# GEGLU MLP, first pass: weight quads from the third on by casting DMA, and half of w_down kept on chip until the down phase

## The chip, the cores and the metric

The kernel runs on one core of a Trainium2 chip. The metric is the device time of one launch in microseconds. A profile is one execution of its own, and its span is about 2 us shorter than the time reported for the same run.

## The reference

Eight batches of 1024 rows (8192 rows in all) of width 1024 go through a gated MLP with an intermediate width of 4096:

```python
gate = x @ w_gate                       # (8192, 1024) @ (1024, 4096)
up = x @ w_up
gate = 0.5 * gate * (1 + np.tanh(np.sqrt(2 / np.pi) * (gate + 0.044715 * gate ** 3)))
h = gate * up
return (h @ w_down).astype(np.float32)  # (8192, 4096) @ (4096, 1024)
```

## The kernel before

The kernel takes the rows in eight passes of 1024. Each pass has a gate/up phase and a down phase. Both multiply block matrices with seven products instead of eight, so sums of weight blocks are operands too, and VectorE makes them. In the first three passes the gate/up phase runs over 16 *pairs* of 14 products; one product is four matmuls of 128x128 by 128x512. A *quad* is the 512 columns of both weights that serve two pairs. Later passes use operands that passes two and three have stored.

The first pass has two extra duties. It has to bring the weights in as fp16 while there is no spare memory, and it has to make the 14 chunks of w_down operands (seven blocks in two halves) that every down phase loads.

Weights, first pass: ScalarE loads eighths of a quad in fp32 and casts them. The casting load of the next two passes is shown with it.

```python
def load_stage(u):                                  # issued on ScalarE
    q, w, k = eighth(u)
    if q < NQ:
        nc.scalar.dma_start(out=staging(u), in_=w_v[w][:, k, q * 512 : (q + 1) * 512])

def cast_stage(u):
    q, w, k = eighth(u)
    if q < NQ:
        nc.scalar.copy(raw(0, q)[:, w, k], staging(u))

def load_raw(p, q):                                 # passes 1 and 2: fp32 to fp16 in the DMA
    if q < NQ:
        for w in range(2):
            nc.gpsimd.dma_start(out=raw(p, q)[:, w], in_=w_v[w][:, :, q * 512 : (q + 1) * 512])
```

w_down, first pass: eight groups, each of four casting loads from GpSimd's queue into one staging tile (`h_s`), four sums on VectorE and seven stores from SyncE's queue.

```python
def wd_load(q, t):
    nc.gpsimd.dma_start(out=hf["s3"][:, t * 1024 : (t + 1) * 1024], in_=wd_v[:, 4 * q + t, :])
# ... wd_sums(k): four sums of 128x1024 on VectorE
def wd_store(q):
    # ...
    for v, src in ((0, b11), (1, b21), (5, b22), (2, tt[:, 0]), (3, tt[:, 1]), (4, tt[:, 2]), (6, tt[:, 3])):
        nc.sync.dma_start(out=dst(v), in_=src)
```

Where they stand, counted in products from the start of the pass (14 to a pair):

```python
for u in range(8):                                   # every quad
    s = (3, 6, 9, 12, 14, 16, 18, 20)[u] + (2 if q == 0 else 0)
    # ... cast eighth 8*(q+1)+u, then load the eighth four further on
for n in range(8):
    s0 = 24 * n + 6
    for ds, f, a in (
        (0, wd_load, (n, 0)), (2, wd_load, (n, 1)), (4, wd_load, (n, 2)), (6, wd_load, (n, 3)),
        (14, wd_sums, (0,)), (15, wd_sums, (1,)), (16, wd_sums, (2,)), (17, wd_sums, (3,)),
        (19, wd_store, (n,)),
    ):
        # ...
```

## Time and profile before

| what | us |
|---|---|
| median of all runs up to the prediction's result (4) | 2335.75 |
| profiled span | 2331.6 |
| TensorE idle in the span | 48 |
| first gate/up pass, pairs 2 to 15 | 194.4 |
| the same 784 matmuls at the second pass's rate | 169.3 |

How to read the profile lines: PE is TensorE, DVE VectorE, ACT ScalarE, POOL GpSimd and SP SyncE; a q behind the name is the engine's sequencer, which among other things issues DMAs. L462 is line 462 of the kernel (the changed kernel has other numbers). `ps` is PSUM, the memory that TensorE writes its products to, used here as eight banks; `tmp` are the temporaries that ScalarE copies them to; `h_s` is the staging tile of w_down and `wd_ops` its operands in device memory. "PE ps L462 <- ACT tmp L473: 11.3, 10, 4.8" says that TensorE waited 11.3 us in all for ScalarE's copy, in 10 waits, the longest 4.8 us.

### The profile page before, as it was taken

To read this page: it belongs to the slowest core of one execution; us is meant where nothing else is said; L and a number is where in the kernel's file an instruction comes from. 1 tells how busy PE (TensorE), PEld (TensorE's weight loads), DVE (VectorE), ACT (ScalarE), POOL (GpSimd) and SP (SyncE) were. 2 spreads that over 40 slices of the span, in tenths; PEclk is the share of its full clock that TensorE was granted. 3 is DMA by queue.
4 is the path that set the end of the run, shared out by engine and by line. 5 is a ranking of instruction groups with operands and counts; after the bars stand their busy time and mean duration, and the time that the engine had idled before them with its cause. 6 is when DMAs were issued, how large, how long until landed. Compare 5 with 4: busy or idle time off the path is not lost.

```text
span 2331.6 us, 38269 instructions
## 1 busy us (share of the span) xinstructions
PE 2283.6 (98%) x14668; PEld 1434.6 (62%) x14668; DVE 1348.8 (58%) x1959; ACT 1015.2 (44%) x1922; POOL 668.6 (29%) x813
## 2 busy tenths in 40 slices
PE   6899999999999999999999999999999999999999
PEld 2334444444444444888558884688747886488854
DVE  4556536775377772576627674466734667356650
ACT  5666215553155530555215551255413654055530
POOL 1222102331033310444205450145402543034520
PEclk9999999999999999999999999999999999999999
DMA  8899778989799885897768876798857988588852
GB/s 268 244 272 275 224 184 206 224 215 296 183 212 257 204 292 200 279 317 271 236 223 289 305 278 207 254 306 288 275 195 260 319 275 265 198 275 276 268 215 108
DMA packets 259942, 579.22 MB, mean 248 GB/s; under 512 B 76016, under 2 KB 119024, under 8 KB 244976
## 3 DMA queue, kind: packets, MB, share of 16 engines
q1 hardware_dynamic: 206080, 490.80, 61.8%
q0 software_dynamic: 38448, 56.63, 14.5%
q10 hardware_dynamic: 15232, 29.36, 3.8%
q8 instruction: 114, 1.87, 0.3%
q14 instruction: 68, 0.56, 0.1%
HBM read 520.09 MB, written 113.25 MB: 272 GB/s over the span
## 4 chain that ended last, share of the span: by engine, by line
PE 90%; DMA 4%; ACT 2%; DVE 1%; issue 1%; ACTq 0%; POOL 0%; SPq 0%; DVEq 0%; POOLq 0%
PE ps L671 39%; PE ps L766 33%; PE ps L462 18%; DMA ring<-in_w_up_dram 1%; ACT ring L260 1%; DMA h_s<-in_w_down_dram 1%; DMA wd_ops<-h_s 1%; ACT tmp L473 1%; DMA h_a<-in_w_gate_dram 1%; DMA h_a<-in_w_up_dram 0%; DVE ring L295 0%; ACTq L253 0%; DMA w_ops<-x_sums 0%; DVE tmp L481 0%; DVE h_a L499 0%
## 5 line engine op out<-in xcount | busy, mean ns | idle before, releaser
L671 PEld LDWEIGHTS <-ring 128*128 128x128 f16 x8320 | 814.1, 98 | 95.2
L648 POOL TENSOR_TENSOR h_a<-tmp 128x256 f16<-128x256 f32 x640 | 465.1, 747 | 927.7 <-ACT tmp L636 893.4
L766 PE MATMUL ps<-ring,h_a 128*128 128x512 f16 x3072 | 665.6, 379 | 0.0
L671 PE MATMUL ps<-x_sums,ring 128*128 128x256 f16 x5760 | 655.8, 273 | 0.0
L633 DVE TENSOR_TENSOR tmp<-tmp,ps 128x512 f32<-128x512 f32 x640 | 413.8, 683 | 219.5 <-PE ps L671 167.9
L766 PEld LDWEIGHTS <-h_a 128*128 128x128 f16 x3072 | 300.6, 98 | 361.4
L462 PEld LDWEIGHTS <-ring 128*128 128x128 f16 x2688 | 263.5, 98 | 354.5 <-issue 42.0
L618 ACT COPY tmp<-ps 128x512 f32<-128x512 f32 x520 | 304.8, 586 | 203.1 <-PE ps L671 130.2
L462 PE MATMUL ps<-x_sums,ring 128*128 128x512 f16 x1536 | 355.4, 381 | 24.9 <-ACT tmp L473 14.4
L636 ACT ACTIVATE tmp<-tmp 128x256 f32<-128x256 f32 x640 | 264.1, 418 | 172.8 <-DVE tmp L631 80.3
L722 ACT ACTIVATE tmp<-ps 128x512 f32<-128x512 f32 x128 | 76.4, 597 | 587.2 <-PE ps L766 587.2
L671 PE MATMUL ps<-x_b,ring 128*128 128x256 f16 x2560 | 305.6, 273 | 0.0
L488 POOL TENSOR_TENSOR h_a<-tmp 128x512 f16<-128x512 f32 x96 | 153.0, 1593 | 435.8 <-ACT tmp L486 332.8
L462 PE MATMUL ps<-x_b,ring 128*128 128x512 f16 x1152 | 265.9, 380 | 2.4 <-ACT ps L478 2.0
L631 DVE TENSOR_TENSOR tmp<-ps,tmp 128x512 f32<-128x512 f32 x240 | 165.4, 689 | 152.2 <-ACT tmp L618 104.8
L726 DVE SCALAR_TENSOR_TENSOR tmp<-ps,tmp 128x512 f32<-128x512 f32 x64 | 44.2, 690 | 305.7 <-ACT tmp L722 262.6
L481 DVE TENSOR_TENSOR tmp<-ps,tmp 128x512 f32<-128x512 f32 x192 | 129.4, 683 | 155.0 <-ACT tmp L473 153.3
L730 DVE TENSOR_TENSOR h_a<-h_a,h_a 128x2048 f16<-128x2048 f16 x96 | 111.1, 1216 | 64.6 <-PE ps L766 64.6
L473 ACT COPY tmp<-ps 128x512 f32<-128x512 f32 x192 | 111.7, 586 | 84.4 <-PE ps L462 71.3
L295 DVE TENSOR_TENSOR ring<-ring 128x1024 f16<-128x1024 f16 x192 | 137.4, 729 | 8.9 <-DMA ring<-in_w_up_dram 8.6
L486 ACT ACTIVATE tmp<-tmp 128x512 f32<-128x512 f32 x96 | 60.3, 628 | 137.5 <-DVE tmp L481 135.6
L766 PE MATMUL ps<-ring,h_s 128*128 128x512 f16 x512 | 111.8, 379 | 0.0
(57 smaller groups left out, 790.3 us busy)
## 6 DMA issues: line engine op xcount, KB each, us to landing
ring<-w_ops SPq DMA_DIRECT2D x480, 512.0 KB, 4.5
ring<-wd_ops SPq DMA_DIRECT2D x112, 1024.0 KB, 5.1
out_dram<-tmp SPq DMA_DIRECT2D x128, 256.0 KB, 2.8
w_ops<-x_sums SPq DMA_DIRECT2D x110, 256.0 KB, 6.3
w_ops<-h_s SPq DMA_DIRECT2D x82, 256.0 KB, 5.7
ring<-in_w_gate_dram POOLq DMA_DIRECT2D x16, 1024.0 KB, 9.8
ring<-in_w_up_dram POOLq DMA_DIRECT2D x16, 1024.0 KB, 18.1
wd_ops<-h_s SPq DMA_DIRECT2D x56, 256.0 KB, 5.8
```

The source lines that it names most:

```text
L295: nc.vector.tensor_tensor(o, a, b, op)
L462: nc.tensor.matmul(ps(b, w), lhs[:, k], rhs[:, k, :], start=(first and k == 0), stop=(k == KH - 1), skip_group_check=True,)
L473: nc.scalar.copy(tl((n, w)), ps("a", w))
L481: nc.vector.tensor_tensor(o, ps("b", w), o, ADD)
L488: nc.gpsimd.tensor_tensor(hq[TO[n]][:, i, :], tmp[:, t[n, 1]], tmp[:, t[n, 0]], MUL)
L618: nc.scalar.copy(tmp[:, t[o[1]]], ps_all[:, bank[o[2]]])
L631: nc.vector.tensor_tensor(d, b, a, SUB)
L633: nc.vector.tensor_tensor(d, a, b, ADD if o[4] == "add" else SUB)
L636: nc.scalar.activation(d, d, GELU, scale=GSC)
L648: nc.gpsimd.tensor_tensor(h, tmp[:, t[o[1]], MQ : 2 * MQ], g, MUL)
L671: nc.tensor.matmul(ps_all[:, bank[c], w * MQ : (w + 1) * MQ], lhs[:, w, k], rhs[:, k], start=(first and w == 0 and k == 0), stop=(k == KH ...
L766: nc.tensor.matmul(ps_all[:, bank[b, g]], lhs[:, j, g * P : (g + 1) * P], dc[:, n, :], start=(first and j == 0), stop=(j == NP - 1), skip_ ...
```

## The change

Its intent is to free ScalarE in the first pass, and to halve the work of making the w_down operands there. The weights from the third quad on come by the casting DMA that the later passes use. Of w_down, only half is staged in the gate/up phase (four groups instead of eight); the other half is loaded at the end of the phase into memory that has become free, and its sums and stores are made during the first down phase.

```diff
     def load_stage(u):
         q, w, k = eighth(u)
-        if q < NQ:
+        if q == 1:
@@ gate_up_one, first pass
-                for u in range(8):
-                    s = (3, 6, 9, 12, 14, 16, 18, 20)[u] + (2 if q == 0 else 0)
+                for u in range(8 if q == 0 else 0):
+                    s = (5, 8, 11, 14, 16, 18, 20, 22)[u]
@@
-                for n in range(8):
-                    s0 = 24 * n + 6
+                if e == 1:
+                    at(13, load_raw, p, q + 2)
+                if 11 <= i < 15:
+                    at(7, half_load, 0, 2 * (i - 11))
+                if i >= 14:
+                    at(4, half_load, 1, 4 * (i - 14))
+                    at(6, half_load, 1, 4 * (i - 14) + 2)
+                for n in range(4):
+                    s0 = 36 * n + 34
@@ down, first pass (cut: half_sum, half_store, half_block and their places)
+        half_work = {
+            (0, 1): [lambda: half_sum(1, 0)],
+            (0, 3): [lambda: half_sum(1, 1)],
+            ...
+            (2, 0): [lambda: half_store(0), lambda: half_store(1)],
+            ...
+        }
@@
+                if p == 0:
+                    if kc == 0:
+                        for k in (2, 4, 6):
+                            load_d(p, k)
+                    load_d(p, {0: 8, 6: 10, 8: 12}.get(kc, 14))
```

More of the change, by code (lines that the diff above doesn't have):

```diff
@@ L131 @@
     wd_v = w_down.rearrange("(nc n) h -> n nc h", n=P)
+    wd_eo = w_down.rearrange("(j e n) h -> e n j h", e=2, n=P)
     xh = nc.dram_tensor("x_half", (M, K), FP16, kind="Internal").ap()
@@ L258, in cast_stage @@
         q, w, k = eighth(u)
-        if q < NQ:
-            nc.scalar.copy(raw(0, q)[:, w, k], staging(u))
+        nc.scalar.copy(raw(0, q)[:, w, k], staging(u))
     def staging0(w, kh):
@@ L373, in wd_store, with half_load, half_block, half_sum @@
             nc.sync.dma_start(out=dst(v), in_=src)
-    order = [[]]
-    def d_chunk(k):
-        o = 4096 * order[0][k % 6]
+    wd_half = [
+        t.rearrange("p (j h) -> p j h", j=8) for t in (xc[:, 8192:16384], rg[:, 0:8192])
+    ]
+    wd_t = [xc[:, j * 4096 : (j + 1) * 4096].rearrange("p (j h) -> p j h", j=8) for j in range(2)]
+    def half_load(e, j):
+        nc.gpsimd.dma_start(out=wd_half[e][:, j : j + 2], in_=wd_eo[e][:, 8 + j : 10 + j, :])
+    def half_block(v):
+        lo, hi = slice(0, HH), slice(HH, 2 * HH)
+        return (
+            wd_half[0][:, :, lo], wd_half[1][:, :, lo], wd_t[1], wd_t[0],
+            wd_half[0][:, :, hi], wd_half[1][:, :, hi], wd_half[0][:, :, lo],
+        )[v]
+    def half_sum(n, r):
+        b11, b21, t2, t1, b12, b22, _ = [half_block(v)[:, 4 * r : 4 * r + 4] for v in range(7)]
+        o, a, b = ((t1, b12, b11), (t2, b22, t1), (b12, b22, b12), (b11, b21, t2))[n - 1]
+        nc.vector.tensor_tensor(o, a, b, SUB)
+    def half_store(v):
+        nc.sync.dma_start(out=wdop[2 * v + 1], in_=half_block(v))
+    order = [[]]
+    def d_place(p, k):
+        if p == 0:
+            return (4, 2, 3, 5, 4, 5, 4)[k // 2]
+        return order[0][k % 6]
+    def d_chunk(p, k):
+        if p == 0 and k % 2:
+            return half_block(k // 2)
+        o = 4096 * d_place(p, k)
         return rg[:, o : o + 4096].rearrange("p (n h) -> p n h", n=8)
-    def load_d(k):
-        if k < 14:
-            nc.sync.dma_start(out=d_chunk(k), in_=wdop[k])
+    def load_d(p, k):
+        if k < 14 and (p or k % 2 == 0):
+            nc.sync.dma_start(out=d_chunk(p, k), in_=wdop[k])
     SEQ = [
@@ L524, in gate_up_one @@
             if p == 0:
-                for u in range(8):
-                    s = (3, 6, 9, 12, 14, 16, 18, 20)[u] + (2 if q == 0 else 0)
+                for u in range(8 if q == 0 else 0):
+                    s = (5, 8, 11, 14, 16, 18, 20, 22)[u]
                     if s // 14 == e:
                         k = s % 14 + 1
-                        at(k, cast_stage, 8 * (q + 1) + u)
-                        at(k, load_stage, 8 * (q + 1) + u + 4)
+                        at(k, cast_stage, 8 + u)
+                        at(k, load_stage, 8 + u + 4)
                 if first:
@@ L565, in gate_up_one @@
                 order[0] = [0, 1, 4, 2, 3, 5] if p % 2 == 0 else [2, 3, 4, 0, 1, 5]
-                at(2, load_d, 0)
-                at(3, load_d, 1)
+                if p:
+                    at(2, load_d, p, 0)
+                    at(3, load_d, p, 1)
             if i == NP - 1:
-                at(1, load_d, 2)
+                at(1, load_d, p, 2 if p else 0)
             pair(p, i, extra, SEQ0 if first else SEQ, AFTER0 if first else AFTER1)
@@ L683, in quad @@
                 if q == NQ - 1 and j % 2 == 1:
-                    load_d(j // 2)
+                    load_d(p, j // 2)
             for f in extra.get(n, ()):
@@ L738, in down @@
             sums["P6", 0, r] = [("a12", "a12", "a11", SUB, r)]
+        half_work = {
+            (0, 1): [lambda: half_sum(1, 0)],
+            (0, 3): [lambda: half_sum(1, 1)],
+            (1, 1): [lambda: half_sum(2, 0)],
+            (1, 3): [lambda: half_sum(2, 1)],
+            (2, 0): [lambda: half_store(0), lambda: half_store(1)],
+            (3, 0): [lambda: half_store(2)],
+            (3, 1): [lambda: half_sum(3, 0)],
+            (3, 3): [lambda: half_sum(3, 1)],
+            (4, 0): [lambda: half_store(3)],
+            (5, 0): [lambda: half_store(5)],
+            (5, 1): [lambda: half_sum(4, 0)],
+            (5, 3): [lambda: half_sum(4, 1)],
+            (6, 0): [lambda: half_store(4)],
+            (7, 0): [lambda: half_store(6)],
+        }
         work = deque()
@@ L759, in down @@
                 kc = 2 * v + nb
-                dc = d_chunk(kc)
+                dc = d_chunk(p, kc)
                 for g in range(G):
@@ L802, in down @@
                         hsum(*s)
+                    if p == 0:
+                        for f in half_work.get((kc, g), ()):
+                            f()
                     if nb == 0 and g == 0 and p + 1 < NPASS:
@@ L810, in down @@
                         work.popleft()()
-                if kc == 0:
-                    for k in range(3, 6):
-                        if p < FAST:
-                            load_d(k)
-                load_d(kc + 6)
+                if p == 0:
+                    if kc == 0:
+                        for k in (2, 4, 6):
+                            load_d(p, k)
+                    load_d(p, {0: 8, 6: 10, 8: 12}.get(kc, 14))
+                else:
+                    if kc == 0 and p < FAST:
+                        for k in range(3, 6):
+                            load_d(p, k)
+                    load_d(p, kc + 6)
                 if p + 1 < FAST:
```

## The prediction

> **What bounds the kernel now.** I read the summary page first. It says that TensorE is the bound nearly everywhere:
>
> ```profile
> PE 2283.6 (98%) x14668; PEld 1434.6 (62%) x14668; DVE 1348.8 (58%) x1959; ACT 1015.2 (44%) x1922; POOL 668.6 (29%) x813
> ```
>
> PE is busy for 2283.6 of 2331.6 us. All that any change to waits can win is the other 48 us, plus stretches at a low clock. The next view is the table by stretches. I chose the boundaries from the matmuls' timeline: the first two pairs of the first gate/up pass, its other fourteen pairs, and the whole gate/up of the second pass.
>
> ```profile
> 34.30:62.60 28.30, 24.38 (x106) 10.27 (x105) 16.61 (x25) 18.26 (x26) 4.74 (x4) 0.96 0.77 247
> 62.60:255.40 192.80, 174.38 (x778) 76.44 (x777) 117.08 (x168) 122.81 (x189) 54.52 (x56) 0.98 0.86 247
> 352.10:545.60 193.50, 193.50 (x898) 87.62 (x896) 146.49 (x222) 112.32 (x184) 64.04 (x44) 1.00 0.89 223
> ```
>
> The columns are length, busy time of PE, PEld, DVE, ACT and POOL, then clock, DMA share and GB/s. The second pass does 896 matmuls in 193.5 us, without idle time: 0.2159 us each, 0.864 us per product of four, 12.1 us per pair. Fourteen pairs (784 matmuls) should take 169.2 us; in the first pass they take 192.8. So **23.6 us** is lost there: 192.80 - 174.38 = 18.4 us of idle time, the rest slow restarts. The second pass already gets its weights by casting DMA, which is what the change brings to the first.
>
> Who ends the waits? PE's waits from 60 to 260 us, then those from 255 us to the end:
>
> ```profile
> PE ps L462 <- ACT tmp L473: 11.3, 10, 4.8
> PE ps L462 <- ACT ps L478: 4.5, 6, 1.4
> PE ps L462 <- DVE tmp L481: 1.1, 1, 1.1
> PE ps L462 <- DVE ring L295: 0.9, 1, 0.9
> ```
>
> ```profile
> PE ps L462 <- DVE tmp L481: 2.4, 1, 2.4
> PE ps L462 <- DMA ring<-in_w_up_dram: 0.4, 1, 0.4
> ```
>
> After the first pass there is almost nothing to win (2.8 us). In it, ScalarE's copies out of PSUM come late. The chain of waits around 80 us shows why the longest comes (4.8 us):
>
> ```profile
> 66.36 1.63 POOL h_s L338 x3
> 67.99 8.07 DMA h_s<-in_w_down_dram
> ...
> 76.54 7.41 DMA wd_ops<-h_s
> ...
> 84.49 0.59 ACT tmp L473
> 85.09 0.04 issue
> 85.13 5.28 PE ps L462 x12
> ```
>
> A load of w_down into the staging tile waits on GpSimd until the previous stores from it have landed. The GpSimd products behind it wait too, so temporaries are not freed, ScalarE can't copy, and PE stops. The other waits follow casts of weight eighths on ScalarE:
>
> ```profile
> L260 ACT CAST ring<-x_sums x56: 1037/1048/1059, 37.7 to 225.7; 128x1024 f16<-128x1024 f32 x56
> ```
>
> **What the Trainium skill says.** (1) "TensorE: Matmul & The Clock Gate", Part 1: the clock halves after an idle window of about 3.4 us. The trace agrees: after the 4.75 us gap at 80 to 85 us the granted clock over 85.1 to 88.5 is 0.50, and 20 matmuls take 7.2 us where 4.3 are due: 2.9 us more. (2) The same page, "Architectural detail": ScalarE and VectorE are strict FIFO, so one sum that waits for a transfer holds up every PSUM operation behind it. The GpSimd case above shows the same shape. (3) "DMA: Bandwidth & Descriptors", "Queues, rings and completion order": descriptors of a ring are consumed in order. All GpSimd transfers here are in one queue, and in the second pass the up half of a weight quad lands 18.4 us (median) after issue, the gate half issued just before it 9.5 to 9.9: one after the other. (4) The same page, "Issuing engines are not separate DMA queues": changing the issuer wins no bandwidth, only issue time. So I expect gains from ScalarE and the waits, not from the bytes; first-pass loads by the other queue run at a DMA share of 0.86 already.
>
> **The change part by part.**
>
> *Weights by casting DMA.* Of 56 casts (1.048 us each) 48 go, and as many DMA issues on ScalarE's sequencer (0.374 us): 50.3 + 18.0 = 68 us of ScalarE's time over pairs 2 to 15. ScalarE then has 122.81 - 50.3 = 72.5 us of work in a 169.2 us stretch, below the second pass's 112.3 in 193.5. Its waits should vanish there.
>
> *w_down.* The staged quarters go from eight to four, spaced 36 products, not 24. From the store to the next load there were 24 - 19 = 5 products (4.3 us) against stores that land in 5.8 us median, 7.4 in the chain; now 17 products (14.7 us). The staging wait, with its 4.75 us and the clock's 2.9, goes. So I credit the whole 23.6 us first.
>
> *The start.* Three w_down loads issued at 1.44 us now come after pair 1. They are 1.57 MB of input beside the 8.4 MB of x and first weights that PE waits for (7.6 us, the longest wait of the start; DMA share about 1.0 from 10 to 30 us). At 346 GB/s in that window, the time for 1.57 MB is 4.5 us; I take **3.5**, as the wait can't shrink by more than what else comes due. Pairs 0 and 1 keep their eight casts but lose four load issues and some DVE sums: **1** more.
>
> *What it adds: new waits on DVE.* A casting load of a quad is 2.1 MB written; queue 0 had 69% of 20.6 us for it, 14 us or 16 products. I place issues by product number (14 per pair). Quads go out at 27, 55, 83, 111, 139, 167; w_down pieces at 34-40, 70-76, 106-112, 142-148; DVE's sums of them stand at 48, 84, 120, 156. Behind a quad on the same ring, with 1.5 us per piece and some 2 us to land:
> - group 0 (behind 27): lands about 51-53, DVE waits 3 to 4 products;
> - group 1: lands 83-87, about 1;
> - group 2: its last piece (112) goes out just after the quad of 111, lands about 131, needed at 121: **DVE waits 10 products, 8.6 us**;
> - group 3 (behind 139): lands 167-169, needed at 156: 11 products, 9.5 us.
>
> PE feels this only once a PSUM bank is missing: product 3 of the next pair needs the bank that the product at the end of this pair (the first h multiply) frees. For group 2 that is product 129, and DVE gets there at about 131 + 2.4 us of work = 134: 5 products, 4.2 us. Group 3: 174 against 171, 2.6 us. Groups 0 and 1 are absorbed. With a clock dip for one of them (1.5): **+8 us**.
>
> *Down phase of pass 0.* PE had no idle in it (448 matmuls in 96.7 us). Added: 8 sums of 128x2048 at 1.22 us = 10 us on DVE, which has slack (19 to 26 busy in 60 us), and seven 1 MB stores in place of seven 1 MB loads. The first chunk is now loaded one pair, not two, ahead (12.1 us against 7.2 median to land), beside the last half loads. I allow **+1** for a late landing, and **+1** for leftover jitter in the pass.
>
> Sum: 2337.3 - 23.6 - 3.5 - 1 + 8 + 1 + 1 = **2319 us**, 0.8% less.
>
> **The rivals.**
> - *All is hidden.* The casting loads run faster beside the few stores of this pass, DVE's waits stay under its slack: no +8. For: the second pass runs with a DMA share of 0.89 and no idle PE. Against: it has no second user of the ring. Time: about 2310.
> - *The ring becomes the bound.* Loads are slower than 14 us (in this pass startup and staging overlap), DVE waits 12 us or more for each of groups 0, 2 and 3, PE stalls 6 to 9 us each and the clock halves each time. For: when stores compete, an up half has taken up to 25.9 us to land (worst, with an x cast between). Against: stores here are half of before. Time: 2330 to 2337, the gain eaten.
> - *The down phase takes it back:* late half loads, or SyncE's queue blocked by the half stores. For: each half store waits for a sum. Against: the loads behind it are needed 27 us later. Cost 2 to 8 us: 2321 to 2327.
> - *Bytes bound the pass.* DMA share 0.86 to 0.9 before; then no gain from PE's waits. Against: the second pass; and 7.3 MB of stores leave the pass.
>
> **Range and chances.** The floor is 2337.3 - 28.1 = 2309 with every wait gone; the bad rival gives about 2335. Range 2309 to 2331. For over 2% faster, 47 us would have to go, and all idle time is 48: 0.01. For over 2% slower, the new waits would have to cost 75 us: 0.02. Within 2%: 0.97.
>
> **What would show each step.** Right: the casts of the first pass number 8; PE's waits on ScalarE's copies after 62 us go from 16 us to under 2; the chain no longer runs through a w_down load, its store and a copy; the second matmul block starts about 3.5 us earlier; DVE shows waits on w_down landings of some 9 us twice, with PE gaps of 3 to 5 us at pairs 9 and 12; the first down phase keeps PE busy. Wrong: no DVE wait on w_down (the ring is faster or shared), a gap at the start of the first down phase, or pass 0 still missing 20 us with PE waiting on a weight load itself.

## The result, and the profile after

The changed kernel took 2318.93 us (median of 4, 2318.51 to 2322.43) against 2335.75 us (median of 4, 2333.29 to 2340.28). The ratio is 0.9929, 95% interval 0.991 to 0.9948. Forecast were 2319 us; the total was right, and so was the class (within 2%). Whether the steps were is another matter.

First the summary page's line of engines, after the change:

```profile
PE 2282.1 (99%) x14668; PEld 1435.2 (62%) x14668; DVE 1350.2 (58%) x1951; ACT 969.9 (42%) x1874; POOL 671.3 (29%) x817
```

TensorE is idle for 34.6 us of the span, 48 before. Where that came from is in the tables by stretch (length; busy PE, PEld, DVE, ACT, POOL; clock; DMA share; GB/s). Before, pairs 2 to 15 of the first pass with the start corrected (this window ends with the last matmul's modelled end, 0.17 us after the next phase has begun):

```profile
60.86:255.44 194.58, 176.16 (x786) 77.22 (x785) 118.82 (x171) 122.85 (x189) 54.52 (x56) 0.98 0.86 249
```

After, the same fourteen pairs, then the first down phase:

```profile
55.90:235.70 179.80, 172.66 (x785) 77.37 (x784) 107.86 (x157) 79.31 (x140) 61.69 (x63) 0.97 0.88 168
235.70:334.30 98.60, 96.88 (x449) 43.78 (x448) 46.97 (x51) 11.88 (x20) 6.18 (x6) 1.00 1.05 251
```

Note the clock (0.97): the pass still loses 10.5 us over the ideal 169.3, about 7 in idle time, the rest at a slow clock. With the starts of the phases read from TensorE's timelines, the ledger is:

| stretch | before | after | change | predicted |
|---|---|---|---|---|
| launch to the end of the second transposes | 34.2 | 30.1 | -4.1 | -3.5 |
| rest of pairs 0 and 1 | 26.7 | 25.8 | -0.9 | -1 |
| pairs 2 to 15 | 194.4 | 179.8 | -14.6 | -23.6 + 8 + 1 |
| first down phase | 96.7 | 98.6 | +1.9 | +1 |
| second gate/up | 193.5 | 194.5 | +1.0 | 0 |
| third gate/up | 197.0 | 199.0 | +2.0 | 0 |
| all the rest | | | -0.2 | 0 |

The changes add up to -14.9 us, which is the difference of the two profiled spans; the medians differ by 16.8.

What ends TensorE's waits after the change, from 60 to 260 us:

```profile
PE ps L496 <- DVE h_a L533: 5.9, 1, 5.9
PE ps L496 <- ACT ps L512: 1.1, 1, 1.1
```

Of the four kinds of wait of before (17.8 us) only one wait for ScalarE's copy is left (1.1 us), and one new gap has come. It ends with VectorE's first h multiply (L533), as the prediction had it for group 2. Follow it back. GpSimd's queue after the change (start, duration, what it issues):

```profile
127.15 1.13 POOL L338 DMA_DIRECT2D h_s<-in_w_down_dram  x2
128.26 0.91 POOL L280 DMA_DIRECT2D ring<-in_w_gate_dram  x1
129.15 0.91 POOL L280 DMA_DIRECT2D ring<-in_w_up_dram  x1
130.02 0.59 POOL L338 DMA_DIRECT2D h_s<-in_w_down_dram  x1
```

One w_down piece is issued behind a whole quad. The view of the w_down loads gives the slowest landing of all of them:

```profile
DMA to landing us min/median/max: 3.8/7.4/16.0
```

130.02 + 16.0 = 146.0 us. VectorE in that time (in brackets: idle before, and the releaser, which the profile could not name here):

```profile
136.86 0.68 DVE L515 TENSOR_TENSOR tmp<-ps,tmp 128x512 f32<-128x512 f32 x1
146.09 0.69 DVE L356 TENSOR_TENSOR h_s<-h_s 128x1024 f16<-128x1024 f16 x1 [8.54 <-issue]
...
147.90 0.69 DVE L533 TENSOR_TENSOR h_a<-ps,tmp 128x512 f16<-128x512 f32 x1
```

The sum at L356 waits 8.54 us, everything behind it waits too, and at 147.90 the multiply at last frees the PSUM bank. TensorE:

```profile
138.29 4.48 PE L496 MATMUL ps<-x_b,ring 128*128 128x512 f16 x20
148.64 1.87 PE L496 MATMUL ps<-x_sums,ring 128*128 128x512 f16 x4 [5.87 <-DVE h_a L533]
151.58 6.63 PE L496 MATMUL ps<-x_sums,ring 128*128 128x512 f16 x20 [1.08 <-ACT ps L512]
```

Four matmuls in 1.87 us instead of the usual 1.03, twenty in 6.63 instead of 4.48: 3.0 us more for the slow clock. With 5.87 + 1.08 us of idle time that is 9.9 of the 10.5 us.

The other groups' waits on VectorE were small:

```profile
DVE h_s L354 <- DMA h_s<-in_w_down_dram: 6.1, 2, 3.3
DVE h_s L356 <- DMA h_s<-in_w_down_dram: 1.2, 2, 0.6
```

These are groups 0 and 3, 3.9 and 3.4 us; TensorE felt neither.

### The profile page after: what moved, and what is told of

The parts are those of the page before. It is cut to its first block, busy times and chain, and to the rows that moved or that the text cites. A ratio compares the mean times of both kernels' runs of the same rounds, so it can differ in the third digit from the quotient of the medians.

```text
span 2316.7 us, 38115 instructions
## 1 busy us (share of the span) xinstructions
PE 2282.1 (99%) x14668; PEld 1435.2 (62%) x14668; DVE 1350.2 (58%) x1951; ACT 969.9 (42%) x1874; POOL 671.3 (29%) x817
## 3 DMA queue, kind: packets, MB, share of 16 engines
q8 instruction: 114, 1.87, 0.3%
## 4 chain that ended last, share of the span: by engine, by line
PE 91%; DMA 3%; DVE 2%; SPq 2%; ACT 1%; issue 1%; POOL 0%; ACTq 0%; DVEq 0%; POOLq 0%
PE ps L713 39%; PE ps L825 32%; PE ps L496 20%; SPq L177 1%; DMA ring<-in_w_up_dram 1%; DVE ring L295 1%; DVE tmp L515 1%; DVE x_sums L200 1%; DMA h_a<-in_w_up_dram 0%; DMA ring<-wd_ops 0%; DMA h_a<-in_w_gate_dram 0%; DVE h_a L533 0%; DMA h_s<-in_w_down_dram 0%; ACT ring L260 0%; ACT tmp L507 0%
## 5 line engine op out<-in xcount | busy, mean ns | idle before, releaser
L825 PE MATMUL ps<-ring,h_a 128*128 128x512 f16 x2944 | 638.3, 379 | 1.7 <-DMA ring<-wd_ops 1.7
L496 PEld LDWEIGHTS <-ring 128*128 128x128 f16 x2688 | 264.2, 98 | 339.8 <-issue 25.8
L522 POOL TENSOR_TENSOR h_a<-tmp 128x512 f16<-128x512 f32 x96 | 147.6, 1538 | 431.4 <-ACT tmp L520 350.5
L825 PE MATMUL ps<-ring,h_s 128*128 128x512 f16 x480 | 104.9, 379 | 0.0
```

The costliest lines, as they stand in the source:

```text
L496: nc.tensor.matmul(ps(b, w), lhs[:, k], rhs[:, k, :], start=(first and k == 0), stop=(k == KH - 1), skip_group_check=True,)
L522: nc.gpsimd.tensor_tensor(hq[TO[n]][:, i, :], tmp[:, t[n, 1]], tmp[:, t[n, 0]], MUL)
L825: nc.tensor.matmul(ps_all[:, bank[b, g]], lhs[:, j, g * P : (g + 1) * P], dc[:, n, :], start=(first and j == 0), stop=(j == NP - 1), skip_ ...
```

## The experiments

Nine kernels ran, each with runs of the kernel before on the same chip. Names are as in the quoted expectations; times are medians, ratios are against the kernel before. The changed kernel was measured in a call of its own, so where two changed kernels are compared, the difference of their ratios is given too: it takes out what differs between calls.

### One load moved ahead of the quad (e1_one_load)

```diff
-(4, wd_load, (n, 2)), (6, wd_load, (n, 3)),
+(4, wd_load, (n, 2)), (4 if n == 2 else 6, wd_load, (n, 3)),
```

> The changed kernel with one load moved: the last w_down piece of group 2 is issued two products earlier, ahead of the weight quad instead of just behind it. Queue-order theory: the piece lands before its sum at product 121, VectorE's 8.5 us wait and TensorE's gap of 5.9 + 1.1 us go, with the slow clock after it; 7 to 8 us faster than the changed kernel, about 2311 us. Rival (bytes: the DMA engines are simply full there): the same bytes cross in the same time, so the wait moves to the quad or to another piece and the time stays within 3 us of 2319.

Measured: 2308.95 us, ratio 0.9896 (0.9881 to 0.9911), so 10 us under the changed kernel by the medians and 8 by the ratios: as the queue-order theory had it, and its number (7 to 8 us) or a little more. Moving one issue of 256 KB by two products (1.7 us) is all that was done. The pass:

```profile
57.10:227.30 170.20, 169.61 (x786) 76.76 (x785) 109.00 (x157) 79.22 (x140) 61.66 (x63) 1.00 0.93 177
```

0.6 us of idle time against 7.1, clock 1.00. The bytes are the same, so the DMA engines being full was not the cause. Group 3's wait on VectorE stays (2.7 + 0.6 us) and costs nothing.

### The sums of that group moved back (e2_sums_later)

```diff
                     ):
+                        if n == 2 and ds >= 14:
+                            ds += 11
                         pr, k = divmod(s0 + ds - 1, 14)
```

> The changed kernel with no load moved, but the four sums and the store of group 2 stand 11 products later in VectorE's order. Theory (TensorE stops because one waiting sum holds the PSUM operations behind it in VectorE's order): the piece still lands some 17 us after issue, VectorE's wait shrinks to under 1 us, TensorE's gap goes, about 2311 us; group 3's first load may be held 1 to 2 us on GpSimd by the later store, without cost. Rival (TensorE stops for the weight quad or the transfers themselves): the gap stays, about 2319.

Measured: 2309.58 us (2304.53 to 2315.1, a wide spread), ratio 0.9896. Here the piece comes as late as in the changed kernel, and the gap is gone all the same; in the chain TensorE runs from 99.9 to 150.2 us in one piece. So the late transfer alone costs nothing: it cost because a waiting sum stood in front of PSUM work. One number was off: VectorE still waits 3.6 us at L356, where under 1 was expected. The piece lands 15.9 us after its issue, as in the changed kernel (16.0); but a sum that waits for no matmul is reached as soon as VectorE has done what stands before it, here sooner than its product number says.

### The first group's loads put back to the start (e3_first_group_early)

```diff
                     ):
+                        if n == 0 and ds < 14:
+                            ds -= 28
                         pr, k = divmod(s0 + ds - 1, 14)
```

> The changed kernel with the loads of w_down group 0 put back where the kernel before has them, so that three go out at about 1.4 us beside the first x and weights. Theory (the three loads cost the start about 4 us of transfer time): first matmul block after the transposes starts 4 us later, at about 34 us, and the whole is 3 to 4 us slower, about 2322.5 (group 0's wait of VectorE goes, but TensorE did not feel it). Rival (the start's 4 us come from something else, such as fewer issues on ScalarE): no change, about 2319.

Measured: 2325.56 us, ratio 0.9963. The matmuls after the second transposes start at 34.28 us against 30.08, the 4.2 us of the theory. The profiled span is 4.3 us over that of the changed kernel (2321.0 against 2316.7), which is these 4.2 us. The medians differ by 6.6 and the ratios by 8 us, over the 3 to 4 expected. The profile is of the fastest of this kernel's four runs, which lie 4 us apart; what the others lost beyond the start isn't shown.

### Chunk 10 of the first down phase (e4_chunk10_place2)

```diff
-            return (4, 2, 3, 5, 4, 5, 4)[k // 2]
+            return (4, 2, 3, 5, 4, 2, 4)[k // 2]
-                    load_d(p, {0: 8, 6: 10, 8: 12}.get(kc, 14))
+                    load_d(p, {0: 8, 2: 10, 8: 12}.get(kc, 14))
```

> The changed kernel with the first down phase's chunk 10 loaded into another place of the ring (free after chunk 2) and issued ahead of the x transposes in SyncE's order. Theory (the 1.7 us wait at chunk 10 comes from its load standing behind transposes and half stores on SyncE): the wait goes, the first down phase takes 96.7 us instead of 98.6, about 2317. Rival (the load is late because the DMA engines are busy): the wait stays or moves to chunk 12, no change.

Measured: 2316.57 us, ratio 0.9927. The medians are 2.4 us under the changed kernel's, but the ratios (0.9927 and 0.9929) differ by less than their intervals: the total doesn't show the gain. The profile does, where it was expected: the first down phase is back at 96.7 us (236.26 to 332.95 us), and no wait for a chunk is left in it. The chain of waits of the changed kernel shows what stood in the way; SyncE had the four x transposes (L177), 28.4 us from 265.82 on, in front of the load of the chunk, which then took 10.9 us:

```profile
277.76 9.22 SPq L177
...
287.04 4.19 SPq L177
...
291.27 2.96 SPq L177
...
295.69 10.87 DMA ring<-wd_ops
306.56 0.14 issue
306.70 5.34 PE ps L825 x24
```

### The weight half of the change alone (e5_casting_alone)

The kernel before, with `load_stage`, the loop over eighths and `load_raw` as in the change, and w_down as before (eight groups, `s0 = 24 * n + 6`).

> The kernel before with the weight half of the change alone: quads from the third on by casting DMA, w_down still in eight groups spaced 24 products, all in the first pass. Queue-order theory: groups 1, 2 and 3 stand behind a quad in the ring when their sums come due, VectorE waits 3 to 8 us for each, and the stores of one group still hold the next one's loads on GpSimd; TensorE loses 10 to 18 us of the 23.6 again, and the start keeps its three loads: 2320 to 2331 us. Rival (the casts on ScalarE were the whole loss): the first pass loses nothing after pair 1, about 2312 us.

Measured: 2331.59 us, ratio 0.9987 (0.9972 to 1.0002): 0.6 us over the upper edge of what the queue-order theory said, and no gain clear of the noise. The casts are gone, and still gate/up from 34.1 us takes 220.7 us, 221.1 before. VectorE now waits for w_down landings, one of them with three pieces ahead of a quad and one behind it:

```profile
DVE h_s L354 <- DMA h_s<-in_w_down_dram: 18.3, 4, 6.4
DVE h_s L356 <- DMA h_s<-in_w_down_dram: 11.0, 4, 8.7
```

TensorE's gaps are 4.1, 6.0, 1.1, 0.7, 2.5 and 1.6 us, with the clock at 0.94 over 60 to 200 us.

### The w_down half alone, first try (e6_four_groups_alone)

```diff
-                for n in range(8):
-                    s0 = 24 * n + 6
+                for n in range(4):
+                    s0 = 36 * n + 34
@@ wd_store; wrong result on purpose
             nc.sync.dma_start(out=dst(v), in_=src)
+            nc.sync.dma_start(out=wdop[2 * v + 1, :, o : o + 2, :], in_=src)
```

> The kernel before with the w_down half alone; a wrong result on purpose: four groups of w_down spaced 36 products, each stored in both halves' places, so half of w_down is never read; the casts stay on ScalarE, as does the staging of the weights. Theory (two causes in the kernel before, the staging wait with its slow clock and the casts): the 4.8 us gap and its slow clock go (7.7 us) and the start's 4 us, while TensorE's short waits on ScalarE's copies stay at 6 to 10 us: about 2319 to 2323 us. Rival (the casts alone cause the waits): only the start's 4 us go, 2330 us.

Measured: 2345.95 us, ratio 1.0047. This missed both theories: slower than before, although the start gained its 4 us. The output is wrong, as meant. The reason stood in ScalarE's waits:

```profile
ACT tmp L474 <- DMA wd_ops<-h_s: 13.1, 3, 8.0
```

ScalarE waits for *stores of w_down*, which it neither reads nor writes. In the chain that the prediction quotes, two of the lines that I had cut between the store and the copy are these:

```profile
83.97 0.02 ACTq L253
...
84.02 0.37 ACTq L253
```

L253 is ScalarE's own issue of a weight load. Its timeline around the gap in the kernel before:

```profile
78.36 1.05 ACT L260 CAST ring<-x_sums 128x1024 f16<-128x1024 f32 x1
84.02 0.37 ACTq L253 DMA_DIRECT2D x_sums<-in_w_up_dram  x1
84.49 1.07 ACT L473 COPY tmp<-ps 128x512 f32<-128x512 f32 x2 [5.09 <-DMA wd_ops<-h_s]
```

After the cast ScalarE does nothing until the issue goes out. In the built program the transfers of SyncE and ScalarE share eight semaphores, DMAHW0 to DMAHW7, on which a transfer signals that it has landed. An issue that uses one again can first have to wait until the last transfer on it has landed, whosever it was. This issue has such a wait, and the trace has the numbers: the wait at 83.97 us is for semaphore 118, on which the load is then issued, and the last to use 118 was SyncE's w_down store of 76.54 us, which took 7.41 us.

GpSimd was not what ScalarE waited for. It had issued its four w_down loads at 66.36 us and finished a product at 77.32; then it waited for ScalarE, not for a store:

```profile
76.05 1.27 POOL L488 TENSOR_TENSOR h_a<-tmp 128x512 f16<-128x512 f32 x1 [2.63 <-ACT tmp L486]
91.70 1.27 POOL L488 TENSOR_TENSOR h_a<-tmp 128x512 f16<-128x512 f32 x1 [14.38 <-ACT tmp L486]
```

So the new theory: the longest gap came from ScalarE, held in its own issue, and not from GpSimd. Two runs tested it.

### Weight loads from GpSimd's queue (e8_loads_from_gpsimd)

```diff
     def load_stage(u):
-            nc.scalar.dma_start(
+            nc.gpsimd.dma_start(
                 out=staging(u), in_=w_v[w][:, k, q * 512 : (q + 1) * 512]
```

> The kernel before with one thing changed: the weight eighths are loaded (still in fp32) from GpSimd's queue, not from ScalarE's; the casts on ScalarE and the eight w_down groups stay. New theory (ScalarE itself was held: its load issues share DMA semaphores with SyncE's w_down stores, and an issue waits until the store that last used the semaphore has landed): ScalarE's waits on the stores go, the 4.8 us gap at 85 us and its slow clock go, the start gains 4 us because the first w_down loads come later on GpSimd: 2318 to 2326 us. Rival (the prediction's: GpSimd is held by the staging wait and does not free the temporaries): GpSimd is held as before or longer, the gap at 80 to 90 us stays, only the start gains: 2330 us or more.

Measured: 2318.26 us, ratio 0.9929 (0.9914 to 0.9944). One word in the kernel before, with all 56 casts still on ScalarE and all eight w_down groups staged, gains as much as the whole change, though not in the same places: 4.0 us at the start, 3.2 in pairs 0 and 1 and 9.2 in pairs 2 to 15, which still take 185.2 us. Nothing is left of the stores in ScalarE's waits, the longest of which (60 to 240 us) are:

```profile
ACT tmp L486 <- DVE tmp L481: 32.2, 14, 4.5
ACT tmp L473 <- PE ps L462: 13.2, 20, 1.2
ACT ring L260 <- DMA x_sums<-in_w_up_dram: 10.7, 8, 4.5
```

The gap at 85 us is gone, and with it the rival: GpSimd is held longer than before (it waits 52.7 us in all for casts that free its staging), and that does no harm of the old kind. The 4.0 us of the start (30.2 us against 34.2) come as w_down's first loads now stand behind weight loads on GpSimd. What remains are waits for ScalarE's copies (11.3 us from 60 to 260 us), the longest (4.1 us) behind a cast that waits for its weights (4.5 us), which come through the same ring as w_down. One rival is left: the edit also takes ScalarE's own issue time away (56 times 0.374 = 21 us), so these runs don't show how much of the gain is that and how much the held issues. That the gap at 85 us was a held issue, the trace of the kernel before shows.

### The w_down half alone, each group stored once (e9_four_groups_one_store)

```diff
-                for n in range(8):
-                    s0 = 24 * n + 6
+                for n in range(4):
+                    s0 = 36 * n + 34
@@ load_d; wrong result on purpose
-            nc.sync.dma_start(out=d_chunk(k), in_=wdop[k])
+            nc.sync.dma_start(out=d_chunk(k), in_=wdop[k - k % 2])
```

> The kernel before with the w_down half alone, as in the run that stored each group twice, but each group stored once and the down phases reading the stored chunk for both; a wrong result on purpose. Casts and load issues stay on ScalarE. New theory (ScalarE's issues wait for the stores): four bursts of seven stores still hold ScalarE, the waits on stores stay in its list at about half, the start gains 4 us: 2322 to 2328 us. Rival (the prediction's: the spacing alone cures the staging wait): no wait on a store on ScalarE, TensorE waits only 6 to 10 us from 60 to 260 us in pieces under 1.5 us: 2317 to 2321 us.

Measured: 2333.26 us, ratio 0.9994 (0.9978 to 1.0011), the result wrong as meant. The wait stays, as the new theory has it:

```profile
ACT ps L478 <- DMA wd_ops<-h_s: 5.8, 1, 5.8
ACT tmp L473 <- DMA wd_ops<-h_s: 3.9, 1, 3.9
```

The wider spacing did not remove it (TensorE's two longest gaps are now 5.7 and 3.2 us), which refutes the prediction's account of the staging wait. But the number was 5 us over the theory's upper edge: the total that ScalarE waits for stores is 9.7 us, not half of before's 6.6. Half the stores in bursts just as long hold it no less; why it is rather more, these runs don't show.

### Both faults mended (e7_groups_before_quads)

The changed kernel with chunk 10 as in e4, and the groups placed so that each stands ahead of a quad and behind one that has landed:

```diff
-                    s0 = 36 * n + 34
+                    s0 = 28 * n + 46
-                        (14, wd_sums, (0,)), (15, wd_sums, (1,)),
-                        (16, wd_sums, (2,)), (17, wd_sums, (3,)), (19, wd_store, (n,)),
+                        (12, wd_sums, (0,)), (13, wd_sums, (1,)),
+                        (14, wd_sums, (2,)), (15, wd_sums, (3,)), (16, wd_store, (n,)),
```

> The changed kernel with its two found faults mended: the four w_down groups spaced 28 products so that every piece stands ahead of a quad, behind one that has landed (sums 12 products after the first piece), and chunk 10 as in the run before. Theory: no wait of VectorE on w_down, no gap of TensorE from pair 2 to the end of the first down phase; the pass takes 169.2 us after pair 1 and the down phase 96.7; 10 us under the changed kernel, 2306 to 2309 us. Rival (with the pieces crowded ahead of the quads, the quads come late for their sums, or GpSimd is held by the stores, 11 products before the next load): a wait on the weight load, 2310 us or more.

Measured: 2305.06 us (2303.67 to 2306.1), ratio 0.9872 (0.9856 to 0.9889), correct: the best of all, 14 us under the changed kernel (13 by the ratios), and 1 us under the theory's range. Pairs 2 to 15, then the first down phase:

```profile
55.10:224.70 169.60, 169.41 (x786) 76.70 (x785) 107.51 (x157) 79.68 (x140) 62.67 (x63) 1.00 0.94 178
224.70:321.40 96.70, 96.70 (x450) 43.85 (x449) 43.78 (x46) 11.86 (x20) 6.18 (x6) 1.00 0.87 242
```

Both phases are at the rate of the later passes. Of the 26.7 us for which TensorE is still idle, 18.8 lie in the first 55 us.

## Why the prediction was right, and where it was not

The total and the class held: 2318.93 us measured, 2319 forecast. That the total fits to 0.1 us is luck. The prediction started from 2337.3 us, the median of the three runs it had, 1.5 us over the later median of four. From there it forecast 18.3 us less; the medians gave 16.8 and the profiles 14.9, and within that several terms were off against each other. Step by step:

- **The start (-3.5).** Right: -4.1, and e3 shows the cause by bringing 4.2 us back. **Pairs 0 and 1 (-1):** -0.9.
- **The credit of 23.6 us.** Right in kind: with every wait gone the pass runs at the second pass's rate (e7). The size was 1.5 us short, as the boundary lay eight matmuls late.
- **Why the longest gap came.** Wrong. The prediction said that GpSimd waits to load into the staging tile and so does not free temporaries, and that the wider spacing cures it. The runs show ScalarE held in its own load issue by a semaphore shared with SyncE's stores: e9 has the spacing and keeps the wait, e8 has only another issuer and loses it. So the GpSimd case, which the prediction also took for an example of in-order queues, isn't one; VectorE's 8.54 us after the change are. The total did not suffer, because the change removes 48 of the 56 issues too: again luck, as the gap went for another reason than the one forecast. With the cut lines of the chain before me I could have seen it; I had left them out as bookkeeping. The prediction counted 18 us of ScalarE's issue time; the waiting in the issues (6.6 us for stores) came on top, and how much of TensorE's loss each made is not shown.
- **The new waits on DVE (+8).** For group 2 they were there as worked out: 8.54 us against 8.6, on the piece that was named, ended by the multiply that was named. The gap of TensorE was larger, 5.9 + 1.1 us and 3.0 of slow clock, not 4.2 + 1.5. For group 3 the term was mis-sized: 3.4 us of VectorE's waiting instead of 9.5, and none of TensorE instead of 2.6. The prediction let the pieces land 28 to 30 products (24 to 26 us) after the quad goes out. Its own terms (16 products for the quad, four pieces at 1.5 us, 2 us to land, the last two not derived there) give only 22 us, and in the trace the first sum's pieces had landed 17.5 us after the quad's issue (161.57 to 179.03 us) and the last 18.8. The two errors nearly cancel, which is luck: 9.9 us against 8 + 1.
- **The down phase (+1).** +1.9, and in another place: not the first chunk, but chunk 10 behind the transposes on SyncE. The nearest rival is the one in which SyncE's queue is blocked. It named the half stores, not the transposes, and was held unlikely because the loads behind were needed 27 us later; 28.4 us of transposes stood before them.
- **Not foreseen:** +3.0 us in the second and third gate/up. Of the +2.0 in the third, 1.7 are one stretch at a slow clock: twenty matmuls take 6.16 us after a gap of 2.37 us. All eleven profiles have that gap (2.37 or 2.44 us) at that place. After it the matmuls are slow (6.12 to 6.16 us) in six: the changed kernel, e1, e2, e3, e6 and e9. In five they take 4.48: the kernel before, e4, e5, e7 and e8. It goes with neither half of the change, so the 1.7 us can't be put down to it; why it comes stays open. Of the other +1.0, 0.6 us are two waits for ScalarE; the rest stays open.

How much each half of the change is worth has no simple answer. Alone, neither gains anything clear of the noise: the weights by casting DMA 0.1% (e5: VectorE waits 29 us for w_down pieces that share the ring with the quads) and the w_down half 0.1% (e9: the issues still hold ScalarE). Together they gain 0.7%, and placed well 1.3%.

## What to carry to other kernels

Before you move loads to another queue, list for each in-order queue what will stand in front of what: a small transfer behind a large one in one ring comes as late as the large one, and a vector operation that waits for it holds all the work behind it. Place the small loads just ahead of the large one, not just after. And when an engine waits for a transfer that it has no business with, look at the issue in front of it: a compute engine that issues DMAs can be held by other queues' transfers through shared semaphores.

## What the Trainium skill lacked or had wrong

- "DMA: Bandwidth & Descriptors", "Issuing engines are not separate DMA queues", says that initiating on several engines only saves the sequencer's time, which is usually small. Here that time was not small for the engine that issues: the weight loads took 21 us of ScalarE's sequencer (56 times 0.374), and moving them to GpSimd's queue, with the same bytes, gave 2318.26 against 2334.49 us, some 4 us of it from the changed order at the start. The page has no word on the time that an issue loses when it waits for another queue's transfer through a shared semaphore (5.09 us in one case here).
- The same page, "Queues, rings and completion order": that a ring is consumed in order, which the section says of the rings of SyncE and ScalarE, agrees with the runs for GpSimd's too. It gives no size for what that costs a small load: a piece of 256 KB behind a quad of 2 MB landed 16.0 us after issue; the median of the w_down loads was 7.4.
- "TensorE: Matmul & The Clock Gate", Part 1, puts the slow clock after an idle window of about 3.4 us. The gaps of 4.75 and 5.87 us agree. But gaps of 2.37 and 2.44 us were also followed by a slow stretch (6.12 to 6.16 us for 20 matmuls) in six of the eleven profiles, and not in the other five (4.48 us).
